# A two-layer trunk in fp32 on one core: every third feed-forward accumulator moved to the small PSUM banks

## The chip, the cores and the metric

The kernel runs on one core of one Trainium2 chip, in one launch. TensorE (PE in the profile, PEld for its weight loads) multiplies into PSUM, eight banks of 512 fp32 columns on each of 128 partitions. VectorE (DVE) and ScalarE (ACT) read the sums from PSUM and write SBUF; GpSimd (POOL) and SyncE (SP) here mostly issue DMAs. The metric is device microseconds of a run; three runs of the kernel before gave a median of 1580.35 us (1576.94 to 1583.97).

## The reference

Two layers work on 640 tokens (512 latent, 128 context) of width 1024. Each layer is an adaLN-modulated RMSNorm, one input projection for three groups of heads (windowed attention, Fourier mixing, latent attention), an output projection with a gated residual, and then the feed-forward, which is what the change touches:

```python
def _conv_ffn(h, w_ug, conv_w, conv_b, w_down):
    u = h @ w_ug                                   # 1024 -> 2 x 2816
    up = jnp.pad(u, ((0, 0), (half, half), (0, 0)))
    uc = sum(up[:, i:i + n] * conv_w[i] for i in range(CONV_W)) + conv_b
    a, g = jnp.split(uc, 2, axis=-1)
    return (jax.nn.silu(g) * a) @ w_down           # 2816 -> 1024
```

The modulation vectors come from `silu(c) @ w_ada + b_ada`, 6144 numbers per layer and condition vector; a part of them is made while the feed-forward runs.

## The kernel before

Activations lie feature-major: a tile is 128 features by 640 tokens. Every fp32 operand is split into a high and a low part (`hh`/`hl`, `th`/`tl`, `wh`/`wl`), and a product is three matmuls (high by high, high by low, low by high), each in two halves of 320 columns, since a bank holds 512. So an accumulator takes two banks, one for each half.

PSUM has two pools. `pmm` holds two tiles "mm" of two banks each; `pss` holds four tiles "s" of one bank each, which serve the attention, the transposes and the row statistics. An `Acc` (line 99) is one "mm" tile, or, with `Acc(False)`, two "s" tiles.

The feed-forward of a layer is the loop at line 338. A step "up" f makes two products, a and g, of feature tile f: eight steps over k, 48 matmuls each. `conv` (line 1278) takes each from PSUM: VectorE multiplies it by the row statistic `r` into `u` (line 1282), ScalarE copies two edge columns (line 1284), which is the last read of the bank, and then come the bias `bb`, the middle tap `y` on ScalarE and the two outer taps on VectorE (line 1292). After g, ScalarE makes the SiLU, VectorE the product `z`, and both split it into `th` and `tl`. A step "down" comes after one more "up" and multiplies a group of six feature tiles (the last group: four) into eight output tiles, 36 matmuls each; `resid` (line 533) adds each to `x` on VectorE in three instructions, the first and only reads of the bank. In the text an accumulator is called a0, g0, a1, g1, ... for the up products and d0 to d7 for the eight output tiles of a down group.

Weights come by DMA in units of up to 128 x 1024 (`wr`, two buffers), and ScalarE and VectorE split each into `wh` and `wl` (lines 186 and 188, four buffers each). VectorE has one more duty in the feed-forward: `ada_dve` (line 350) makes 48 rows of modulations in layer 0 and 8 in layer 1, two reductions over 1024 elements per row ("junk", line 364). The tuple `CFG[l]["ada"]` says how many are asked for after each up step; in layer 0 also each output tile of a down step asks for one, in layer 1 all eight are done by then.

The order on each engine is set by the framework's scheduler, which walks the program by priority with a cost table of its own and gives out the pools' buffers as they come free in its own time. Each engine then runs its list strictly in order and waits by semaphores. At the end of a layer the last down group runs by halves of tokens (`tail`, line 604): in between, `Norm.sums` (line 433) adds the squares by three small matmuls, ScalarE and VectorE make the inverse root (`rc`, line 376), VectorE puts it on a diagonal (`diag`, line 382), and `Norm.spread` (line 442) broadcasts it by three more matmuls. The next layer's first product needs that.

Of the kernel before, what the change touches and what calls it, by code (L numbers as in the profile page):

```python
# [21 lines left out]
HF = 320  # L22
# [56 lines left out]
def hybrid_step(ctx: ExitStack, tc: tile.TileContext, I, O):  # L79
    nc = tc.nc  # L80
# [12 lines left out]
    def MM():  # L93
        return pmm.tile([128, 2, 512], F32, tag="mm", name="mm")

    def PS():
        return pss.tile([128, 512], F32, tag="s", name="s")

    class Acc:


        def __init__(s, wide=True, hfs=(0, 1)):
            s.wide = wide
            if wide:
                s.t = MM()
                s.h = [s.t[:, hf, :] for hf in range(2)]
            else:
                s.h = [PS()[:, :HF] if hf in hfs else None for hf in range(2)]

        def pieces(s):  # L110
            if s.wide:
                return [(s.t[:, :, :HF], halves)]
            return [(s.h[hf], lambda ap, hf=hf: ap[:, hf * HF:(hf + 1) * HF]) for hf in range(2)]

    def SM(name, w=4, bufs=4):
        return sm.tile([128, w], F32, tag=name, name=name, bufs=bufs)
# [1 line left out]
    def halves(ap):  # L118
        return ap.rearrange("p (a b) -> p a b", a=2)
# [4 lines left out]
    def acopy(out, in_):  # L124
        return nc.scalar.activation(out, in_, AF.Copy)  # L125
# [133 lines left out]
    def P(l, n):  # L259
        return pk[l][:, PK[n][0]:PK[n][1]]  # L260
# [972 lines left out]
    if True:  # L1233
# [18 lines left out]
        nrm = Norm(x, 0, 0)  # L1252
# [3 lines left out]
        for l in range(L):  # L1256
            u = U[l]

            def begun():
                x.clear()  # L1260
                i = nc.vector.tensor_scalar_mul(nsink[:, l], P(l, "sink"), -1.0)
                if l:
                    tc.keep_in_program_order(i)

            xn, nrm = mixer(l, nrm, begun, I["xT"] if l == 0 else xd)


            hs = nrm.hs()
            cv = P(l, "conv").rearrange("p (t q) -> p t q", q=4)
            T = {}  # L1270
            bg = ada_dve(0, [(0, n) for n in range(40, 48)] + [(1, n) for n in range(40)]) if l == 0 else ada_dve(48, [(1, n) for n in range(40, 48)])
            made = 0

            nws = SM("nws", 2 * NFT, 1)
            nc.vector.reduce_sum(out=nws, in_=cv[:, :, 0:3], axis=AX.X)
            nc.vector.tensor_scalar_mul(nws, nws, -1.0)

            def conv(ps, t):
                uu = S("u", w=UW)
                for c0, c1, o, p in ((0, NL, 0, 1), (CX, NT, 256, 515)):  # L1280
                    n = c1 - c0
                    nc.vector.tensor_mul(halves(uu[:, p:p + n]), ps.t[:, :, o:o + n // 2], halves(nrm.r[:, c0:c1]))  # L1282
                for v, o in enumerate((uu[:, 0:514:513], uu[:, 514:644:129])):
                    acopy(o, ps.t[:, 1, HF + v:HF + v + 1].to_broadcast([128, 2]))
                bb = SM("bb", 2)
                nc.vector.scalar_tensor_tensor(out=bb, in0=uu[:, 513:515], scalar=nws[:, t:t + 1], in1=cv[:, t, 3:4].to_broadcast([128, 2]), op0=ALU.mult, op1=ALU.add)  # L1286
                y = S("y", w=UW)
                for v, (c0, c1) in enumerate(((0, 513), (513, TW))):
                    nc.scalar.activation(y[:, c0:c1], uu[:, c0 + 1:c1 + 1], AF.Identity, bias=bb[:, v:v + 1], scale=cv[:, t, 1:2])  # L1289
                yy = y[:, :TW]  # L1290
                for q in (0, 2):
                    nc.vector.scalar_tensor_tensor(out=yy, in0=uu[:, q:q + TW], scalar=cv[:, t, q:q + 1], in1=yy, op0=ALU.mult, op1=ALU.add)  # L1292
                return yy

            ya = {}

            def cb_a(f):
                def go(ps):
                    ya[f] = conv(ps, 2 * f)
                return go  # L1300

            def cb_g(f):
                def go(ps):
                    y = conv(ps, 2 * f + 1)
                    a = ya.pop(f)
                    nc.scalar.activation(y, y, AF.Silu)  # L1306
                    if f == NFT - 1:
                        nc.scalar.activation(SM("root", 1, 1), y[:, 1:2], AF.Sqrt, bias=eps[:, 0:1], scale=0.0)
                    z = S("z")
                    for c0, c1, o in ((0, NL, 0), (CX, NT, 2)):  # L1310
                        nc.vector.tensor_mul(z[:, c0:c1], a[:, c0 + o:c1 + o], y[:, c0 + o:c1 + o])
                    T[f] = tuple(S(n, F32R) for n in ("th", "tl"))
                    hilo(T[f][0], T[f][1], z)
                return go

            fin = l == L - 1
            nxt = Norm(xn, None if fin else l + 1, 0)
            if fin:
                yout = {}

                def hfin(hf, c):
                    if c not in yout:
                        yout[c] = S("yo")
                    sl = slice(hf * HF, (hf + 1) * HF)
                    nc.vector.scalar_tensor_tensor(out=yout[c][:, sl], in0=xn[c][:, sl], scalar=P(0, "gfin")[:, c:c + 1], in1=nxt.r[hf][:, :HF], op0=ALU.mult, op1=ALU.mult)  # L1325
                    nc.sync.dma_start(out=O["y"][c, :, sl], in_=yout[c][:, sl])

            def upd_d(last):
                def go(c, ps, hfs):
                    resid(xn[c], ps, l, 5, c, hfs)  # L1330
                    if last:
                        for hf in hfs:
                            nxt.sq(c, hf)
                        if not fin and 1 in hfs:
                            nc.gpsimd.dma_start(out=xd[c], in_=xn[c])
                return go

            for kind, a in u["plan"]:
                if kind == "up":
                    for q, cb in (("a", cb_a(a)), ("g", cb_g(a))):  # L1340
                        ps = Acc()
                        drain(dense(W.get(u[q, a]), hs, range(8), ps, True, True, n=UW))
                        cb(ps)
                    for _ in range(CFG[l]["ada"][a] if a < len(CFG[l]["ada"]) else 0):
                        made += next(bg, 0)
                    continue
                while made < 8:
                    made += next(bg)
                f0, f1 = GROUPS[a]
                nk = f1 - f0  # L1350
                ts = tuple({k: T[f0 + k][q] for k in range(nk)} for q in range(2))
                last = a == len(GROUPS) - 1
                up = upd_d(last)
                if not last:
                    for c in range(8):
                        ps = Acc()
                        drain(dense(W.get(u["d", a, c]), ts, range(nk), ps, True, True))
                        up(c, ps, (0, 1))
                        next(bg, None)
                else:  # L1360
                    drain(bg)
                    accs = [Acc(), Acc(), Acc(False)]
                    for ks in (range(nk - 1), range(nk - 1, nk)):
                        for c in range(3):
                            drain(dense(W.get(u["dl", c // 2]), ts, ks, accs[c], ks[0] == 0, ks[0] != 0, off=(c % 2) * nk))
                            if ks[0]:
                                up(c, accs[c], (0, 1))
                    ps = Acc()
                    drain(dense(W.get(u["dl", 1]), ts, range(nk), ps, True, True, off=nk))
                    up(3, ps, (0, 1))  # L1370
                    items = [(c, W.get(u["dl", c // 2], 3 - c // 4), range(nk), (c % 2) * nk) for c in range(4, 8)]
                    done = 0
                    for i in tail(nxt, items, ts, up):
                        upto = CFG[l]["next"][i]
                        for c in range(done, upto):
                            if fin:
                                hfin(0, c)
                            else:
                                nxt.h(0, c)
                        done = upto  # L1380
                    if fin:
                        nxt.stats(1)
                        for c in range(done, 8):
                            hfin(0, c)
                        for c in range(8):
                            hfin(1, c)
                for f in range(f0, f1):
                    T.pop(f)
            nrm = nxt
# [123 lines left out]
```

## Time and profile before

| | us |
|---|---|
| median of three runs | 1580.35 |
| the profiled execution | 1582.09 |
| its span, first to last instruction | 1580.3 |
| TensorE matmul busy | 1525.2 (97%) |
| VectorE busy | 1116.7 (71%) |
| ScalarE busy | 712.3 (45%) |
| mean granted TensorE clock | 0.984 |

The span goes, in order, through the mixer of layer 0 (to about 340 us), its feed-forward (to about 788), the last down group and the change of layers (to about 820), the mixer of layer 1 (to about 1090), its feed-forward (to about 1545) and the end. TensorE's busy share is near the whole span, and a matmul's row overlaps the next one's, so the rows to look for are those where TensorE was idle before an instruction, and who released it. The clock column is the share of full speed that was granted.

### The profile page before, as it was taken

What the parts mean: (1) busy time and instruction counts of PE and PEld (TensorE: products, weight loads), DVE (VectorE), ACT (ScalarE), POOL (GpSimd) and SP (SyncE); (2) the same over time, 40 slices, a digit from 0 to 9 for tenths busy, and PEclk for the clock granted to TensorE, in tenths of its full rate; (3) what the DMA queues carried; (4) which work ended last, traced back from release to release, by engine and by line L of the source; (5) the groups of instructions that cost most, each with busy time, mean ns of one, the idle gap of its engine ahead of it and who ended that gap; (6) DMA issues with size and microseconds to landing.
All of it is one profiled execution on the core that took longest, in us unless ns stands there. A gap on an engine that the chain in (4) does not pass through costs nothing. (4 is left out here: it accounts for less than half of the span.)

```text
span 1580.3 us, 25827 instructions
## 1 busy us (share of the span) xinstructions
PE 1525.2 (97%) x10082; PEld 1426.3 (90%) x10082; DVE 1116.7 (71%) x2257; ACT 712.3 (45%) x1403; POOL 103.7 (7%) x225
## 2 busy tenths in 40 slices
PE   9999989899999999999999999989999999999997
PEld 7977775599999999999999887869999999999997
DVE  5765674477897888889778777867885466466366
ACT  4555664564432432441445666646433243244142
POOL 1200111100000000001011000120000000000000
PEclk9999999899999999999999999999999999999998
DMA  9542239113334335235244202331332222221211
GB/s 363 166 145 74 73 98 312 56 54 120 116 124 169 120 104 196 104 104 193 81 142 133 72 25 86 114 142 54 120 99 75 81 74 61 94 77 52 100 54 67
DMA packets 61800, 177.59 MB, mean 112 GB/s; under 512 B 7360, under 2 KB 9856, under 8 KB 61680
## 3 DMA queue, kind: packets, MB, share of 16 engines
q1 hardware_dynamic: 44112, 116.41, 22.1%
q0 software_dynamic: 17568, 59.55, 11.2%
q8 instruction: 79, 1.29, 0.3%
q14 instruction: 41, 0.34, 0.1%
HBM read 165.02 MB, written 10.91 MB: 111 GB/s over the span
## 5 line engine op out<-in xcount | busy, mean ns | idle before, releaser
L278 PE MATMUL mm<-hh,wh 128*128 128x320 f32 x1632 | 377.5, 312 | 12.3 <-ACT u L125 9.1
L278 PE MATMUL mm<-hl,wh 128*128 128x320 f32 x1632 | 377.2, 310 | 0.7 <-DVE hl L486 0.4
L278 PE MATMUL mm<-hh,wl 128*128 128x320 f32 x1632 | 376.9, 310 | 0.0
L125 ACT ACTIVATE wh<-wr 128x1024 fp32r<-128x1024 f32 (+2 forms) x189 | 185.9, 984 | 343.1 <-PE mm L278 263.9
L278 PEld LDWEIGHTS mm<-hh,wh 128*128 128x128 f32 x1632 | 273.8, 188 | 20.6 <-ACT u L125 11.0
L278 PEld LDWEIGHTS mm<-hl,wh 128*128 128x128 f32 x1632 | 275.6, 188 | 4.0 <-issue 2.1
L278 PEld LDWEIGHTS mm<-hh,wl 128*128 128x128 f32 x1632 | 274.5, 188 | 3.3 <-issue 3.3
L188 DVE TENSOR_TENSOR wl<-wr,wh 128x1024 fp32r<-128x1024 f32 (+2 forms) x187 | 210.9, 1128 | 48.2 <-ACT wh L125 47.3
L1292 DVE SCALAR_TENSOR_TENSOR y<-u,pk,y 128x642 f32<-128x642 f32 x176 | 156.2, 887 | 67.9 <-ACT y L1289 64.2
L278 PE MATMUL mm<-th,wh 128*128 128x320 f32 x656 | 152.4, 310 | 0.0
L278 PE MATMUL mm<-th,wl 128*128 128x320 f32 x656 | 152.2, 309 | 0.0
L278 PE MATMUL mm<-tl,wh 128*128 128x320 f32 x656 | 152.0, 309 | 0.0
L537 DVE SCALAR_TENSOR_TENSOR x<-mm,mod,x 128x192 f32<-128x192 f32 (+2 forms) x222 | 84.9, 435 | 70.6 <-PE mm L278 70.6
L364 DVE CUSTOM_DVE_ANT_0 junk<-wa,sbc 128x1024 bf16<-128x1024 f32 x112 | 132.1, 1223 | 1.8 <-DMA wa<-in_wat 1.8
L1289 ACT ACTIVATE y<-u,bb,pk 128x513 f32<-128x513 f32 (+1 forms) x176 | 105.9, 650 | 60.8 <-DVE bb L1286 60.8
L278 PEld LDWEIGHTS mm<-th,wh 128*128 128x128 f32 x656 | 110.3, 188 | 0.7 <-ACT th L125 0.4
L278 PEld LDWEIGHTS mm<-th,wl 128*128 128x128 f32 x656 | 110.4, 188 | 0.0
L278 PEld LDWEIGHTS mm<-tl,wh 128*128 128x128 f32 x656 | 110.4, 188 | 0.0
L1282 DVE TENSOR_TENSOR u<-mm,r 128x512 f32<-128x512 f32 (+1 forms) x176 | 79.6, 486 | 42.2 <-PE mm L278 40.1
L125 ACT ACTIVATE u<-mm 128x2 f32<-128x2 f32 x176 | 20.8, 170 | 112.5 <-DVE u L1282 107.5
L1306 ACT ACTIVATE y<-y 128x642 f32<-128x642 f32 x44 | 32.6, 741 | 73.7 <-DVE y L1292 73.7
L361 POOL DMA_DIRECT2D wa<-in_wat x56 | 29.5, 528 | 524.2 <-DVE mod L364 517.8
(311 smaller groups left out, 2195.6 us busy)
## 6 DMA issues: line engine op xcount, KB each, us to landing
wr<-in_wug SPq DMA_DIRECT2D x88, 512.0 KB, 3.5
wa<-in_wat POOLq DMA_DIRECT2D x56, 512.0 KB, 3.8
wa<-in_wa SPq DMA_DIRECT2D x80, 256.0 KB, 5.7
wr<-in_wdn SPq DMA_DIRECT2D x48, 384.0 KB, 3.1
wr<-in_wi SPq DMA_DIRECT2D x16, 512.0 KB, 3.7
wr<-in_wo SPq DMA_DIRECT2D x14, 512.0 KB, 3.7
xpart<-xp POOLq DMA_DIRECT2D x16, 320.0 KB, 3.7
x<-xpart POOLq DMA_DIRECT2D x16, 320.0 KB, 6.1
```

The lines of the kernel that those rows point to most:

```text
L125: return nc.scalar.activation(out, in_, AF.Copy)
L188: pin(self.eng.tensor_sub(lo, r, f32(hi)), fix)
L278: pin(nc.tensor.matmul(ps.h[hf][:, :c1 - c0], lhsT=w[wi][:, off[k] if isinstance(off, dict) else k + off, :], rhs=hs[hi][k][:, c0:c1], sta ...
L361: nc.gpsimd.dma_start(out=t, in_=I["wat"][i0 + i])
L364: nc.vector.tensor_tensor_reduce(out=junk, in0=t, in1=sb[v], scale=1.0, scalar=0.0, op0=ALU.mult, op1=ALU.add, accum_out=mod[l][:, n, v:v ...
L537: nc.vector.scalar_tensor_tensor(out=xc[:, c0:c1], in0=ps.h[hf][:, o:o + c1 - c0], scalar=mod[l][:, gidx * 8 + c, v:v + 1], in1=xc[:, c0:c ...
L1282: nc.vector.tensor_mul(halves(uu[:, p:p + n]), ps.t[:, :, o:o + n // 2], halves(nrm.r[:, c0:c1]))
L1289: nc.scalar.activation(y[:, c0:c1], uu[:, c0 + 1:c1 + 1], AF.Identity, bias=bb[:, v:v + 1], scale=cv[:, t, 1:2])
L1292: nc.vector.scalar_tensor_tensor(out=yy, in0=uu[:, q:q + TW], scalar=cv[:, t, q:q + 1], in1=yy, op0=ALU.mult, op1=ALU.add)
L1306: nc.scalar.activation(y, y, AF.Silu)
```

## The change

In the feed-forward, the accumulators of the up steps and of the first three down groups now come from a counter `FA`: two of three are an "mm" tile as before, every third is two "s" tiles. That is 68 accumulators per layer, of which 22 are of the new kind (14 of up steps, 8 of down steps). For these `conv` reads two tiles, so its two multiplications (512 and 128 columns, both halves in one access pattern) become four (two of 256, two of 64). The last down group keeps its own `Acc` calls. `Acc` now keeps whole "s" tiles, because the edge columns lie behind column 320.

```diff
             else:
-                s.h = [PS()[:, :HF] if hf in hfs else None for hf in range(2)]
+                s.h = [PS() if hf in hfs else None for hf in range(2)]
...
-            return [(s.h[hf], lambda ap, hf=hf: ap[:, hf * HF:(hf + 1) * HF]) for hf in range(2)]
+            return [(s.h[hf][:, :HF], lambda ap, hf=hf: ap[:, hf * HF:(hf + 1) * HF]) for hf in range(2)]
...
                     n = c1 - c0
-                    nc.vector.tensor_mul(halves(uu[:, p:p + n]), ps.t[:, :, o:o + n // 2], halves(nrm.r[:, c0:c1]))
+                    if ps.wide:
+                        nc.vector.tensor_mul(halves(uu[:, p:p + n]), ps.t[:, :, o:o + n // 2], halves(nrm.r[:, c0:c1]))
+                    else:
+                        for hf in range(2):
+                            d = hf * n // 2
+                            nc.vector.tensor_mul(uu[:, p + d:p + d + n // 2], ps.h[hf][:, o:o + n // 2], nrm.r[:, c0 + d:c0 + d + n // 2])
                 for v, o in enumerate((uu[:, 0:514:513], uu[:, 514:644:129])):
-                    acopy(o, ps.t[:, 1, HF + v:HF + v + 1].to_broadcast([128, 2]))
+                    acopy(o, ps.h[1][:, HF + v:HF + v + 1].to_broadcast([128, 2]))
...
+            bank = [0]
+
+            def FA():
+
+                bank[0] += 1
+                return Acc(bank[0] % 3 != 0)
...
                     for q, cb in (("a", cb_a(a)), ("g", cb_g(a))):
-                        ps = Acc()
+                        ps = FA()
...
                     for c in range(8):
-                        ps = Acc()
+                        ps = FA()
```

The scheduler's lists move too, though the program text around the change does not. Three places follow; line numbers of the changed kernel are a few higher (1282 there is 1283 and 1287).

VectorE in the first down group of layer 0, the stretch that ends with the split of the weights of d5. Before, it comes after the residual of d1 (`x` is the residual, "ISA junk" a reduction, `wl` the split):

```order
L144 TENSOR_TENSOR tl<-z,th 128x640
L364 ISA junk,mod_87<-wa,sbc 128x1024
L364 ISA mod_87 128x1
L364 ISA junk,mod_87<-wa,sbc 128x1024
L364 ISA mod_87 128x1
L364 ISA junk,mod_87<-wa,sbc 128x1024
L364 ISA mod_87 128x1
L364 ISA junk,mod_87<-wa,sbc 128x1024
L364 ISA mod_87 128x1
L537 SCALAR_TENSOR_TENSOR x<-mm,mod_86,x 128x320
L537 SCALAR_TENSOR_TENSOR x<-mm,mod_86,x 128x192
L537 SCALAR_TENSOR_TENSOR x<-mm,mod_86,x 128x128
```

The next row there is the `wl` of d5. In the change the same four reductions and the residual of d1 come first, and the list goes on like this, with the residuals of d2 ("mm") and d3 ("s"):

```order
L537 SCALAR_TENSOR_TENSOR x<-mm,mod_86,x 128x192
L537 SCALAR_TENSOR_TENSOR x<-mm,mod_86,x 128x128
L364 ISA junk,mod_87<-wa,sbc 128x1024
L364 ISA mod_87 128x1
L364 ISA junk,mod_87<-wa,sbc 128x1024
L364 ISA mod_87 128x1
L537 SCALAR_TENSOR_TENSOR x<-s,mod_86,x 128x320
L537 SCALAR_TENSOR_TENSOR x<-s,mod_86,x 128x192
L537 SCALAR_TENSOR_TENSOR x<-s,mod_86,x 128x128
L364 ISA junk,mod_87<-wa,sbc 128x1024
L364 ISA mod_87 128x1
L364 ISA junk,mod_87<-wa,sbc 128x1024
```

The `wl` of d5 stands right behind this last reduction: it has moved back by two residuals and six reductions. The second and third down group of layer 0 show nearly the same list.

TensorE at the change of layers, from the sums of squares on; before:

```order
L436 MATMUL s<-ones,acc 128x2 x3
L278 MATMUL mm<-th,wl 128x320
L278 MATMUL mm<-th,wh 128x320
L278 MATMUL mm<-tl,wh 128x320
L278 MATMUL mm<-th,wl 128x320
L383 MATMUL s<-diag,ones 128x128
```

Now:

```order
L278 MATMUL mm<-th,wl 128x320
L278 MATMUL mm<-th,wh 128x320
L278 MATMUL mm<-tl,wh 128x320
L278 MATMUL mm<-th,wl 128x320
L436 MATMUL s<-ones,acc 128x2 x3
L383 MATMUL s<-diag,ones 128x128 x2
L383 MATMUL s<-diag,ones 128x64
```

The four matmuls that stood between the sums and the spread have moved ahead of the sums, and the eight that stood between the spread's first and second matmul have moved behind it.

VectorE at the same place; before, the chain from the inverse root (`rc`) to `diag` runs at once:

```order
L537 SCALAR_TENSOR_TENSOR x<-mm,mod_86,x 128x128
L377 RECIPROCAL rc<-rc 128x6
L382 TENSOR_SCALAR diag<-ident,rc 128x128
L429 TENSOR_TENSOR acc<-acc,sq 128x320
L537 SCALAR_TENSOR_TENSOR x<-mm,mod_86,x 128x192
L537 SCALAR_TENSOR_TENSOR x<-mm,mod_86,x 128x128
L382 TENSOR_SCALAR diag<-ident,rc 128x128 x2
L188 TENSOR_TENSOR wl<-wr,wh 128x1024
```

Now:

```order
L537 SCALAR_TENSOR_TENSOR x<-mm,mod_86,x 128x192
L537 SCALAR_TENSOR_TENSOR x<-mm,mod_86,x 128x128
L188 TENSOR_TENSOR wl<-wr,wh 128x1024
L429 TENSOR_TENSOR acc<-acc,sq 128x320
L377 RECIPROCAL rc<-rc 128x6
L429 TENSOR_TENSOR acc<-acc,sq 128x320
L382 TENSOR_SCALAR diag<-ident,rc 128x128 x3
```

The residual, the split of a weight unit and two additions now stand ahead of `diag`.

## Rows read from the trace of the kernel before

**Rows 1.** Page, busy time by engine.
```profile
PE 1525.2 (97%) x10082; PEld 1426.3 (90%) x10082; DVE 1116.7 (71%) x2257; ACT 712.3 (45%) x1403; POOL 103.7 (7%) x225
```

**Rows 2.** Waits, PE and PEld, whole span: total us, times, longest.
```profile
PE mm L278 <- ACT u L125: 9.1, 7, 1.4
...
PEld mm L278 <- ACT u L125: 11.0, 7, 1.7
```

**Rows 3.** Timeline of PE, 371 to 375: start, us, [idle before <-releaser].
```profile
371.68 0.46 PE L278 MATMUL mm<-hl,wh 128*128 128x320 f32 x2
371.97 0.45 PE L278 MATMUL mm<-hh,wl 128*128 128x320 f32 x2
373.86 0.57 PE L278 MATMUL mm<-hh,wh 128*128 128x320 f32 x2 [1.44 <-ACT u L125]
374.26 0.46 PE L278 MATMUL mm<-hl,wh 128*128 128x320 f32 x2
```

**Rows 4.** Timeline of DVE and ACT in the same stretch.
```profile
368.07 1.22 DVE L364 CUSTOM_DVE_ANT_0 junk<-wa,sbc 128x1024 bf16<-128x1024 f32 x1
...
372.65 0.89 DVE L1282 TENSOR_TENSOR u<-mm,r 128x512 f32<-128x512 f32 x2
...
372.17 1.06 ACT L125 ACTIVATE wh<-wr 128x1024 fp32r<-128x1024 f32 x1 [5.38 <-PE mm L278]
```

**Rows 5.** Windows, both feed-forwards: us; PE, PEld, DVE, ACT, POOL busy; PEclk; DMA.
```profile
340.00:785.00 445.00, 439.73 (x2990) 438.69 (x2990) 365.07 (x636) 165.21 (x295) 24.27 (x46) 1.00 0.38 128
1092.00:1540.00 448.00, 444.13 (x3013) 443.29 (x3012) 278.90 (x470) 167.24 (x297) 3.17 (x6) 1.00 0.24 81
```

**Rows 6.** Lines by form, VectorE, line 1282: busy us, mean ns.
```profile
L1282 DVE TENSOR_TENSOR u<-mm,r 128x512 f32<-128x512 f32 x88 | 60.7, 689 | 42.2 <-PE mm L278 40.1 <-ACT r L125 2.0
...
L1282 DVE TENSOR_TENSOR u<-mm,r 128x128 f32<-128x128 f32 x88 | 24.9, 283 | 0.0
```

**Rows 7.** Timeline of DVE, first down group of layer 0.
```profile
446.05 0.69 DVE L1282 TENSOR_TENSOR u<-mm,r 128x512 f32<-128x512 f32 x1 [1.02 <-PE mm L278]
...
449.94 1.81 DVE L1292 SCALAR_TENSOR_TENSOR y<-u,pk,y 128x642 f32<-128x642 f32 x2 [0.40 <-ACT y L1289]
...
455.29 1.22 DVE L364 CUSTOM_DVE_ANT_0 junk<-wa,sbc 128x1024 bf16<-128x1024 f32 x1
...
459.87 1.14 DVE L537 SCALAR_TENSOR_TENSOR x<-mm,mod,x 128x320 f32<-128x320 f32 x3
460.91 0.96 DVE L188 TENSOR_TENSOR wl<-wr,wh 128x768 fp32r<-128x768 f32 x1
...
475.47 1.23 DVE L364 CUSTOM_DVE_ANT_0 junk<-wa,sbc 128x1024 bf16<-128x1024 f32 x1 [0.44 <-DMA wa<-in_wat]
```

**Rows 8.** Timeline of PE, then DVE, at the change of layers.
```profile
812.31 0.73 PE L436 MATMUL s<-ones,acc 128*128 128x2 f32 x6
...
813.94 0.49 PE L383 MATMUL s<-diag,ones 128*128 128x128 f32 x2 [0.21 <-DVE diag L382]
...
819.64 0.56 PE L278 MATMUL mm<-hh,wh 128*128 128x320 f32 x2 [1.24 <-ACT hh L468]
...
813.37 0.19 DVE L377 RECIPROCAL rc<-rc 128x6 f32<-128x6 f32 x1 [0.96 <-ACT rc L376]
...
813.80 0.49 DVE L429 TENSOR_TENSOR acc<-acc,sq 128x320 f32<-128x320 f32 x1
814.20 0.67 DVE L537 SCALAR_TENSOR_TENSOR x<-mm,mod,x 128x192 f32<-128x192 f32 x2
...
815.17 1.22 DVE L188 TENSOR_TENSOR wl<-wr,wh 128x1024 fp32r<-128x1024 f32 x1
```

**Rows 9.** PE idle in the mixer of layer 0, and windows there: PE busy, PEclk.
```profile
282.69 1.48 PE L286 MATMUL mm<-CKb,CQ 96*128 96x320 f32 x5 [2.04 <-ACT P L1105]
...
282.00:288.00 6.00, 5.31 (x27) 0.72 0.00 0
302.00:312.00 10.00, 7.95 (x38) 0.66 0.46 176
```

## The prediction, on record before the changed kernel ran

> **What bounds the kernel now.** The page comes first: TensorE is busy for 1525.2 of 1580.3 us [rows 1], so the change can give back only what TensorE loses by waiting, and the matmuls themselves are as many as before. The view of waits says where that is. In the feed-forwards there is one kind of any size: the first matmul of an accumulator waits for ScalarE's edge copy `u`, the last read of the bank that it wants. That happens 7 times, 9.1 us of idle matmul queue, or 11.0 us seen from the weight loads [rows 2].
>
> The timeline shows what such a wait costs. Pairs of matmuls start every 0.29 us (371.68, 371.97); the next starts at 373.86, which is 1.89 later, and the one after it needs 0.40 instead of 0.29 [rows 3]. So 1.60 + 0.11 = 1.7 us are lost where the row says 1.44, and that is why the weight loads' 11.0 us are the better sum for all seven.
>
> Next, why the bank was late. The accumulator a1 was complete when g1 began, about 365.2 (g1 ends at 372.27, less 24 pairs of 0.295, 7.07 us). But VectorE was in four reductions from 368.07 to 372.65, and only then took a1 out of its bank [rows 4]. With two accumulators, a2 wants a1's bank just when g1 is done: TensorE has 7.07 us of patience, and VectorE came after 7.45. The places fit the program: the tuple asks for two rows of reductions at once after up steps 0, 4, 9 and 15 of layer 0 and 0, 2 and 4 of layer 1, seven in all. Elsewhere TensorE does not wait, and VectorE is busy for 365 of 445 us in layer 0 and 279 of 448 in layer 1 [rows 5]: late at places, not too slow.
>
> **The change part by part.** *A third accumulator.* With two of three on "mm", an "mm" tile is wanted again by the third accumulator after it, so its readers have two whole products, 14.1 us, instead of 7.07; an "s" pair is wanted six later. The longest that a reader took, about 8.6 us (365.2 to the restart at 373.86), fits with 5 us to spare. All seven waits go: -11.0 us. What could be late next is the weights, and in the up steps they are not: ScalarE's split waits for TensorE to free one of the four buffers [rows 4], so weights are as far ahead as the buffers allow.
>
> *Four multiplications for two.* 512 columns take 689 ns and 128 take 283 [rows 6], so a column costs (689 - 283) / 384 = 1.06 ns and an instruction 148 ns before its first column. 28 up accumulators (14 a layer) with two more instructions each are 8.3 us of VectorE, spread over 893 us in which it has 249 us free. On the path: 0, covered by the 14.1 us. If a place had no cover it would cost 0.3 us there.
>
> *The down groups of layer 0.* Here the moved list matters. The weights of d5 are now split behind the residuals of d2 and d3 and six more reductions. I count from the end E of g6 on TensorE (before: 446.0, [rows 7]). TensorE begins d5 after five outputs of 18 pairs, E + 26.5. Before, the split was done at 460.91 + 0.96 = E + 15.9, over 10 us early. Now VectorE can begin with the residual of d0 at E + 5.35. The nine instructions from there to `tl` are the same as those from 449.94 to 455.29, 5.35 us; as the split no longer stands between `z` and `tl`, `tl` waits for ScalarE's `th`, an estimate of 0.8 (ScalarE's split of 1024 columns takes 1.06 [rows 4], this one has 640): E + 11.5. Four reductions, 4.58 (455.29 to 459.87): 16.1. The residual of d1, 1.04: 17.1. Then d2 with two reductions, 1.04 + 2.29, two more, 2.29, d3, 1.04, two more, 2.29: E + 25.8 to 26.1. The split itself, 0.96: E + 26.9. TensorE is 0.4 us late, and with a restart like that of rows 3 it loses 0.7. The other two groups have nearly the same list: 3 x 0.7 = +2.1 us. It is a small difference of two large sums: at best nothing is late (0), and with a reduction that waits for its DMA (0.44 in [rows 7]) and as much error again in the sum, 2 us each (6.0). I take 2.1, the sum itself. In layer 1 the reductions are over by then: 0.
>
> *The change of layers.* Before, TensorE did four matmuls between the sums and the spread and idled 0.21 us; the sums began at 812.31, the reciprocal at 813.37, the spread at 813.94 [rows 8]. Now the spread follows the sums at once, and VectorE has more ahead of it. From the start S of the sums: the residual of the product just ended, from 0.2, takes 0.6 (814.20 to 814.79 or so); the split 1.14; an addition 0.4 (813.80 to 814.20); the reciprocal 0.23; an addition 0.4; the diagonal 0.25: S + 3.2. The sums are done at S + 0.6, so TensorE idles 2.6 us. Part of that is not lost, because before it idled 1.24 us at 819.64 for `hh` [rows 8]. S is now 0.6 later (four matmuls moved ahead), 812.9; spread at 816.1, done at 816.7; twelve matmuls to 818.5; the residual, `ht` and `hh` behind them, 0.6 + 0.5 + 0.6 us: the next layer begins at about 820.3, 0.65 late, and with the weight split that now stands between two of its first steps 0.9. That is the price by the chain alone.
>
> An idle of this length also touches the clock. After the 2.04 us of idle before 282.69 the granted clock was at its lower level for a while, a mean of 0.72 over 6 us, 1.7 us of lost work; around another such idle it was 0.66 over 10 us, 3.4 us [rows 9]. The feed-forward windows with the waits of up to 1.44 us stand at 1.00 [rows 5]. So I add 1.7: 0.9 + 1.7 = +2.6. The bounds are 0.6 (no fall, the split hidden) and 0.9 + 3.4 = 4.3.
>
> [...]
>
> Sum: -11.0 + 2.1 + 2.6 = -6.3 us. Against the profiled execution's 1582.09 us (span 1580.3 and 1.8 around it) that is 1575.8. The profiled run lies 1.7 above the median of the three runs, so as a median I expect 1580.35 - 6.3 = 1574.0 us.
>
> **The rivals.** *Both prices stay hidden.* The first split is late by only 0.4 us of 26.9, and the idle at the layers' change could end up in the 1.24 that was there. Then the seven waits are the whole story: 1580.35 - 11.0 = 1569.4, or 1570 with the chain's 0.6. For it: the sums for the prices are as small as their errors. Against: the moved lists are there, and every idle over 2 us that I looked at was followed by the lower clock.
>
> *The waits only change their name.* If VectorE's reductions delayed the next weights or `tl` as much as the bank, TensorE would stop at the same seven places, and the time would stay at 1580. For it: the split of a unit stands right behind the late `u`. Against: ScalarE's wait for a free weight buffer [rows 4], three units of lead.
>
> *Slower: the clock falls in the down groups.* VectorE gets to the split of d5 at E + 28.3 instead of 26.9, for instance by one more DMA wait and one more late residual. TensorE then idles about 2 us, which is where the rows show the clock fall, in each of three groups: 3 x (2.1 + 3.4) = 16.5, and the change of layers costs its upper bound, 4.3: 1580.35 - 11.0 + 16.5 + 4.3 = 1590. It decides from an idle of 2 us on, that is from 1.4 us more delay than I count. Against: each output adds only 1.04 + 2.29 + 0.87 = 4.2 us to VectorE in TensorE's 5.3, so a delay shrinks again and does not build up.
>
> **How the numbers follow.** About 0.5%, 7.9 us, is what a measurement of this kernel can tell from no change. The forecast, 1574.0, gets 0.50, with a range of its own of 1571 to 1578; hidden prices, 1569.4, 0.25; waits that change their name, 1580, 0.18; slower, 1590, 0.07. Faster by more than 0.5% means below 1572.4: all of the second case and a fifth of the first, 0.35. Slower means above 1588.3: most of the last, 0.05. The rest, 0.60, is within. The range runs from 1567 (hidden prices and 2 us of scatter between runs) to 1582 (the same waits under another name); it leaves out the slow case and the tails.
>
> **What would show it.** Right: no row of PE in the feed-forwards that waits for ScalarE's `u`; in layer 0 three short waits of PE for `wl`, 0.3 to 1 us, at the fifth or sixth output of each of the first three down groups, none in layer 1; a wait of 2 to 3 us for `diag` at the change of layers with the clock below 1.00 behind it. Wrong: `u` still in the waits, waits for `wl` in the up steps, or idles of 2 us in the down groups.

## The result, and the profile after

The changed kernel took 1572.9 us, the median of seven runs (1569.57 to 1573.79), beside 1580.41 of the kernel before on the same chip: a ratio of 0.9947, with a 95% interval of 0.9933 to 0.9961. That is -8.4 us (-10.6 to -6.2). The forecast was 1574.0, -6.3. Measured once more in the last experiment, the change came to 0.9957 (0.9939 to 0.9976), -6.8 us.

TensorE's idle time in the profile fell from 55.1 to 48.4 us (span less busy time); the rest of the difference is busy time. It was longer at the lower granted clock: the second profile of the changed kernel has the same idle time within 1 us (49.2) at a mean granted clock of 0.982 instead of 0.988, and 1524.4 us busy instead of 1519.4. The page's row of busy time, and the windows of the two feed-forwards (us; PE, PEld, DVE, ACT, POOL busy; granted clock; DMA), which answer to [rows 1] and [rows 5]:

```profile
PE 1519.4 (97%) x10082; PEld 1422.0 (91%) x10082; DVE 1118.0 (71%) x2313; ACT 709.8 (45%) x1403; POOL 103.4 (7%) x225
...
340.00:785.00 445.00, 444.39 (x3022) 443.33 (x3021) 368.69 (x667) 164.29 (x298) 24.27 (x46) 1.00 0.38 128
1085.00:1540.00 455.00, 455.00 (x3097) 454.67 (x3096) 287.82 (x515) 173.41 (x309) 3.17 (x6) 1.00 0.24 79
```

In the feed-forwards TensorE is now busy for 444.4 of 445 us and 455 of 455. The seven waits for `u` [rows 2] are gone from PE's waits. The same view for PEld (total us, times, longest), first the whole span and then the feed-forward of layer 0, shows what stands in their place. The one wait for `u` that is left there, 0.3 us, comes at 784.04, behind the up steps; PE's own row shows no idle for it.

```profile
PEld s L383 <- DVE diag L382: 3.8, 2, 2.9
...
PEld mm L278 <- DVE wl L188: 1.4, 3, 0.8
...
PEld mm L278 <- ACT u L125: 0.3, 1, 0.3
```

The three waits for `wl` are one in each of the first three down groups, as the weight loads' timeline (start, us, what waited) shows:

```profile
468.53 0.30 PEld L278 LDWEIGHTS mm<-th,wl 128*128 128x128 f32 x2 [0.27 <-DVE wl L188]
...
596.46 0.30 PEld L278 LDWEIGHTS mm<-th,wl 128*128 128x128 f32 x2 [0.78 <-DVE wl L188]
...
728.76 0.30 PEld L278 LDWEIGHTS mm<-th,wl 128*128 128x128 f32 x2 [0.34 <-DVE wl L188]
```

The change of layers, PE first and then DVE, answers to [rows 8]:

```profile
806.44 0.81 PE L436 MATMUL s<-ones,acc 128*128 128x2 f32 x6
810.06 0.88 PE L383 MATMUL s<-diag,ones 128*128 128x128 f32 x6 [2.81 <-DVE diag L382]
810.75 0.39 PE L278 MATMUL s<-th,wh 128*128 128x320 f32 x1
...
814.21 0.30 PE L278 MATMUL s<-th,wl 128*128 128x320 f32 x1
814.58 0.56 PE L278 MATMUL mm<-hh,wh 128*128 128x320 f32 x2
...
806.64 0.68 DVE L537 SCALAR_TENSOR_TENSOR x<-mm,mod,x 128x192 f32<-128x192 f32 x2 [0.28 <-PE mm L278]
807.58 1.22 DVE L188 TENSOR_TENSOR wl<-wr,wh 128x1024 fp32r<-128x1024 f32 x1 [0.27 <-ACT wh L125]
808.73 0.48 DVE L429 TENSOR_TENSOR acc<-acc,sq 128x320 f32<-128x320 f32 x1
809.13 0.18 DVE L377 RECIPROCAL rc<-rc 128x6 f32<-128x6 f32 x1
809.31 0.49 DVE L429 TENSOR_TENSOR acc<-acc,sq 128x320 f32<-128x320 f32 x1
809.72 0.67 DVE L382 TENSOR_SCALAR diag<-ident,rc 128x128 f32<-128x128 f32 x3
```

TensorE idles 2.81 us for `diag`, behind the residual, the split and the two additions on VectorE. After the spread all 24 last matmuls follow without a pause, and the wait for `hh` (1.24 before) is gone.

Where the time went, by five points of TensorE's timeline: the first matmul of each feed-forward, the sums of squares at the end of each layer, and layer 1's first matmul. The sums stand 0.59 us (four matmuls) later in the changed list; the table takes that off the feed-forward and puts it to the change of layers. The last column is the second profile of the changed kernel.

| stretch, us | before | after | difference | after, again |
|---|---|---|---|---|
| mixer of layer 0 | 341.74 | 339.70 | -2.04 | 341.18 |
| feed-forward of layer 0 | 470.57 | 466.15 | -4.42 | 465.78 |
| change of layers | 7.33 | 8.73 | +1.40 | 11.10 |
| mixer of layer 1 | 271.48 | 269.77 | -1.71 | 272.12 |
| feed-forward of layer 1 | 469.16 | 463.72 | -5.44 | 463.73 |
| end | 20.02 | 19.73 | -0.29 | 19.69 |
| span | 1580.3 | 1567.8 | -12.5 | 1573.6 |

The two profiles alone would say -12.5, 4 us more than the runs. The mixers make up 3.75 of that, where nothing was changed: the granted clock fell in them in both profiles, to a mean of 0.96 over the mixer of layer 0 in each, and of 0.97 before and 0.99 after over that of layer 1. In the windows before and after round the same place of layer 1's mixer it is 0.90 and 0.95 (us; PE busy, granted clock, DMA):

```profile
940.00:975.00 35.00, 33.64 (x196) 0.90 0.23 75
```

```profile
934.00:969.00 35.00, 33.31 (x201) 0.95 0.23 74
```

The second profile of the changed kernel has a longer mixer in layer 1 than before has. What belongs to the change is -4.42 + 1.40 - 5.44 = -8.5 us in the first profile and -4.79 + 3.77 - 5.43 = -6.5 in the second, beside -8.4 and -6.8 of the runs. Each is one execution against the one profile of before, so the agreement is no closer than the clock's price at the change of layers allows (below).

### The profile page after: what moved, and what is told of

It is laid out like the page before. It is cut to its first block, busy times and chain, and to the rows that moved or that the text cites. A ratio compares the mean times of both kernels' runs of the same rounds, so it can differ in the third digit from the quotient of the medians.

```text
span 1567.8 us, 25828 instructions
## 1 busy us (share of the span) xinstructions
PE 1519.4 (97%) x10082; PEld 1422.0 (91%) x10082; DVE 1118.0 (71%) x2313; ACT 709.8 (45%) x1403; POOL 103.4 (7%) x225
## 5 line engine op out<-in xcount | busy, mean ns | idle before, releaser
L278 PE MATMUL mm<-hl,wh 128*128 128x320 f32 (+1 forms) x1184 | 275.0, 310 | 0.9 <-DVE hl L469 0.5
L278 PE MATMUL mm<-hh,wh 128*128 128x320 f32 (+1 forms) x1184 | 273.7, 311 | 1.8 <-ACT wh L125 0.9
L278 PE MATMUL mm<-hh,wl 128*128 128x320 f32 (+1 forms) x1184 | 274.3, 310 | 0.0
L278 PEld LDWEIGHTS mm<-hl,wh 128*128 128x128 f32 x1184 | 199.9, 188 | 4.2 <-issue 2.1
L278 PE MATMUL s<-hh,wh 128*128 128x320 f32 x480 | 111.1, 310 | 0.0
L278 PE MATMUL s<-hh,wl 128*128 128x320 f32 x480 | 111.0, 309 | 0.0
L278 PE MATMUL s<-hl,wh 128*128 128x320 f32 x480 | 110.8, 309 | 0.0
L537 DVE SCALAR_TENSOR_TENSOR x<-mm,mod,x 128x320 f32<-128x320 f32 (+1 forms) x174 | 66.5, 432 | 48.6 <-PE mm L278 48.4
L278 PEld LDWEIGHTS s<-hl,wh 128*128 128x128 f32 x480 | 81.0, 188 | 0.0
L278 PEld LDWEIGHTS s<-hh,wh 128*128 128x128 f32 x480 | 80.9, 188 | 0.0
L278 PEld LDWEIGHTS s<-hh,wl 128*128 128x128 f32 x480 | 80.7, 188 | 0.0
```

The costliest lines, as they stand in the source:

```text
L278: pin(nc.tensor.matmul(ps.h[hf][:, :c1 - c0], lhsT=w[wi][:, off[k] if isinstance(off, dict) else k + off, :], rhs=hs[hi][k][:, c0:c1], sta ...
L537: nc.vector.scalar_tensor_tensor(out=xc[:, c0:c1], in0=ps.h[hf][:, o:o + c1 - c0], scalar=mod[l][:, gidx * 8 + c, v:v + 1], in1=xc[:, c0:c ...
```

## The experiments

| run | what it is | ratio to before, 95% interval |
|---|---|---|
| e1 | third accumulator in layer 1 alone | 0.9990 (0.9975 to 1.0004) |
| e2 | in layer 0 alone | 0.9988 (0.9972 to 1.0004) |
| e3 | before, reductions replaced by a copy | 0.9970 (0.9953 to 0.9986) |
| e4 | changed kernel, the same | 0.9938 (0.9916 to 0.9960) |
| e9 | before, reductions replaced by a memset | 0.9935 (0.9914 to 0.9955) |
| e5 | before, reductions handed out singly | 0.9952 (0.9934 to 0.9969) |
| e6 | changed kernel, all 88 products split | 0.9958 (0.9944 to 0.9972) |
| e7 | changed kernel, longer idle | 1571.87 us, one run |
| e8 | e5 with the sums asked for earlier | 0.9949 (0.9931 to 0.9967) |
| e10 | singly, and earlier; two accumulators | 0.9932 (0.9912 to 0.9953) |
| e11 | the same with the third accumulator | 0.9932 (0.9910 to 0.9953) |
| e12 | the changed kernel again | 0.9957 (0.9939 to 0.9976) |

### One layer at a time (e1, e2)

```diff
-                return Acc(bank[0] % 3 != 0)
+                return Acc(l != 1 or bank[0] % 3 != 0)
```

(e2: `l != 0`.)

> The third accumulator in the feed-forward of layer 1 alone; layer 0 and the change of layers keep the order of before. Theory A (the gain is the waits for a late bank and nothing else, the extra multiplications are covered): the three waits for u at the start of layer 1's feed-forward go, the four of layer 0 stay, no wait for wl is added; -5.4 us, 0.9966 of before. Rival B (the gain comes from the new order as a whole or from the clock): the time does not follow the waits; anything from 1.000 to 0.995.

> The third accumulator in the feed-forward of layer 0 alone, with the new order at the change of layers. Theory A: the four waits for u of layer 0 go, three waits of weight loads for wl (1.4 us in all) and the wait of 2.8 us for diag stand as in the changed kernel; layer 0's feed-forward is 6.5 us shorter, the change of layers 1.4 longer, so -5.1 us, 0.9968 of before, and the three waits of layer 1 stay. Rival B: the sum of this and the run on layer 1 alone differs from the change's 8.4 us by more than 3 us.

The waits came as theory A had them. PE's waits in the two feed-forwards and the change of layers between them, e1 and then e2:

```profile
PE mm L278 <- ACT u L125: 5.3, 4, 1.4
```

```profile
PE mm L278 <- ACT u L125: 3.9, 3, 1.4
PE s L383 <- DVE diag L382: 2.8, 1, 2.8
...
PE mm L278 <- DVE wl L188: 0.4, 1, 0.4
```

In e1 the four waits of layer 0 stay and layer 1's feed-forward takes 464.52 us (469.16 before, -4.6; -5.4 was expected). In e2 the three of layer 1 stay, and layer 0's feed-forward is 4.6 shorter (466.60 less 0.59, against 470.57; 6.5 was expected). The run times did not follow as well. In e2's profile the clock fell after the idle for `diag` (a window of 0.86, below), the change of layers took 9.70 + 0.59 = 10.29 us, 3.0 more than before, and -4.6 + 3.0 = -1.6 lies beside the measured -1.9 (-4.4 to +0.6). That is consistent, but does not show why the median came out there: the profiled execution (1572.48 us) was the fastest of the twelve, its mixer of layer 0 5 us shorter than before's, and without the fall -4.6 + 1.4 = -3.2 would lie in the interval as well. For e1 -4.6 was to be had, and -1.6 (-3.9 to +0.6) was measured. Its profile shows no new wait that would take the 3 us; the mixer of layer 0 was 1.8 longer in it, and at the change of layers its clock fell (0.89 in the window from 814 to 826). By the letter of rival B (the two runs add up to more than 3 us less than the change) B stands; by the rows, and by e5, e9 and e10 below, A does. What slowed e1's runs, and with it this part of B, stays open.

### Without the reductions (e3, e4, e9)

```diff
-            for v in range(2):
-                junk = sp.tile([128, 1024], BF16, tag="S", name="junk")
-                nc.vector.tensor_tensor_reduce(...)
+            nc.vector.tensor_copy(mod[l][:, n, :], t[:, 0:2])   # e3, e4
+            nc.vector.memset(mod[l][:, n, :], 0.0)              # e9
```

> The kernel before with the two reductions of every modulation row in the feed-forwards left out (a copy of two numbers stands for them, so those modulations are not computed; their DMAs stay). Theory A (two accumulators are enough wherever VectorE has no block of four reductions): no wait for u is left, no wait for wl, the change of layers as before: -11.0 us, 0.993. Rival C (u is late by VectorE's whole load, the blocks only make it show): some of the seven waits stay at less than 1.7 us each, 0.995 to 0.999.

> The changed kernel with the same reductions left out. Theory A: the third accumulator has nothing left to give, so the same as the kernel before without reductions within 0.1% (0.993 of before), with no wait for u or wl in either feed-forward; the four multiplications for two cost nothing. Rival D (an accumulator in two small banks costs something of its own, in restarts or in multiplications): 0.5 us or more in each feed-forward, 0.994 or above, against the kernel before without reductions.

> The kernel before with the reductions left out and a memset in their place that reads no row (so those modulations are zero), in place of the copy that waited for the row's DMA in the earlier run without reductions. Theory A (two accumulators are enough when VectorE is not held up): no wait for u in either feed-forward, the change of layers as before, so layer 0's feed-forward about 464.8 us to the sums (before 470.6), layer 1's 463.9 (before 469.2): -11 us, 0.993 of before. Rival C (VectorE's load as a whole): waits for u remain.

e3 missed its forecast for a reason of its own, and a useful one. Two waits for `u` stayed in its layer 0. DVE's timeline shows that the copies, with no reductions to take up the time, stood waiting for their rows' DMA, and held up all behind them; the two PE rows are what came of it, and the clock fell around the longer one (window from 398 to 412: 0.76):

```profile
383.62 0.17 DVE L362 COPY mod<-wa 128x2 f32<-128x2 f32 x1 [2.18 <-DMA wa<-in_wat]
...
400.67 0.17 DVE L362 COPY mod<-wa 128x2 f32<-128x2 f32 x1 [2.78 <-DMA wa<-in_wat]
...
386.87 0.56 PE L278 MATMUL mm<-hh,wh 128*128 128x320 f32 x2 [1.34 <-ACT u L125]
403.93 0.91 PE L278 MATMUL mm<-hh,wh 128*128 128x320 f32 x2 [2.64 <-ACT u L125]
```

e4 had the same copies and the same stalls, one of them longer, and TensorE did not wait in that place:

```profile
398.18 0.17 DVE L362 COPY mod<-wa 128x2 f32<-128x2 f32 x1 [3.67 <-DMA wa<-in_wat]
```

So the third accumulator covered a VectorE that was late by a DMA as well as one that was late by reductions. It was not complete: against the expectation one wait for `u` of 0.2 us stayed in e4's feed-forward of layer 0. In e9, where nothing reads the row, two accumulators have no wait in either feed-forward (464.35 and 463.88 us), and 0.9935 is the expected 0.993. e4's 0.9938 is the same within the noise (its feed-forwards take 464.99 and 463.91), so with the reductions gone the third accumulator gives nothing, and rival D's price in each feed-forward is not there. It is the reductions that make the bank late. Whether their blocks do it or the load that they add (rival C) e9 cannot tell, since it takes away both; e5 and e10 can.

### Reductions one at a time, two accumulators (e5, e8, e10), and with the third (e11)

```diff
-CFG[0]["ada"] = (3, 1, 1, 1, 2, 1, 1, 1, 1, 2, 1, 1, 1, 1, 1, 2, 1, 1, 1, 1)
+CFG[0]["ada"] = (4, 3, 3, 3, 2, 2, 2, 2, 2, 2, 2, 2, 2, 2, 2, 2, 2, 2, 2, 2, 2, 2)   # e5, e8
+CFG[0]["ada"] = (4, 3, 3, 3, 3, 3, 3, 3, 3, 3, 3, 3, 2, 2, 2, 2, 2, 2, 0, 0, 0, 0)   # e10, e11
-CFG[1]["ada"] = (3, 1, 2, 1, 2)
+CFG[1]["ada"] = (4, 3, 3, 3, 2, 2)
-CFG[0]["tail"] = (1, 2)
+CFG[0]["tail"] = (0, 1)   # e8 alone
...
             for v in range(2):
+                if v:
+                    yield 0.5
...
-            yield 1
+            yield 0.5
...
-                    for _ in range(CFG[l]["ada"][a] if a < len(CFG[l]["ada"]) else 0):
-                        made += next(bg, 0)
+                        w = CFG[l]["ada"][a] if a < len(CFG[l]["ada"]) else 0
+                        for _ in range(w // 2 if q == "a" else w - w // 2):
+                            made += next(bg, 0)
...
                         next(bg, None)
+                        next(bg, None)
```

> The kernel before, all accumulators as there, but the reductions handed out one at a time: after each a and each g product, mostly one, never more than two together, and the first eight rows done by up step 5. Theory A: with no block of four VectorE is never later than the 7.07 us of patience, so all seven waits go without another bank: -11.0 us in the feed-forwards; the order at the change of layers comes out like that of the changed kernel, +1.4: 0.994 of before, as the change itself. No waits for wl in the down groups, so up to 2 us better than the change. Rival C (VectorE's load as a whole): waits for u remain, some in new places, 0.997 or above.

> The spread reductions on two banks as before (one at a time), and the sums and the spread of the last down group asked for one item earlier (tail 0, 1 instead of 1, 2), which puts the reciprocal ahead of one addition and the three diagonals ahead of another on VectorE. Theory A: the wait for diag falls from 2.8 to about 2.0 us; the way from the sums to layer 1's first matmul is 0.8 us shorter than in the run without this, the rest the same: 0.9935 of before. Rival: what diag gains hh loses, no difference within 0.1%.

> The kernel before, two accumulators, with the reductions handed out one at a time as in the earlier run, but more of them in the early up steps and none in the last four, which leaves the order at the change of layers as it was before (four matmuls between the sums and the spread, the diagonal ahead of the weight split). Theory A: no wait for u, none for wl, diag 0.2 us and hh 1.24 us as before, clock 1.00 there: -11 us, 0.993 of before, 2.5 us better than the changed kernel. Rival: a wait in a new place in the down groups, where the first rows are wanted, or the price at the change of layers is not the clock's and the time stays at the change's 0.995.

> The same hand-out of reductions, with the third accumulator of the change on top. Theory A: nothing is left for it to give, the same time as two accumulators with this hand-out within 0.1%. Rival G (the third accumulator also covers what the replay of one profile does not show, a late DMA or a slow VectorE place): 1 us or more better than two accumulators.

e5 has no wait of PE for `u` or `wl` with before's banks and all of before's reductions, so rival C falls: the block is what counts. The feed-forwards take 465.11 (465.70 less 0.59) and 463.88 us. It pays at the change of layers, where its list is that of the changed kernel, and comes out where the change does; the 2 us that it might have been better are not there. e8 moved the reciprocal ahead there: the idle is 1.95 us instead of 2.46, and the way from the sums to layer 1's first matmul 8.61 instead of 9.27, 0.66 of the expected 0.8. That is too little for the runs to tell, which gave 0.9949 where 0.9935 was expected. e10 kept before's order there. PE's rows at the change of layers, with the pause for `diag` back at 0.21:

```profile
804.73 0.74 PE L438 MATMUL s<-ones,acc 128*128 128x2 f32 x6
806.37 0.49 PE L385 MATMUL s<-diag,ones 128*128 128x128 f32 x2 [0.21 <-DVE diag L384]
...
812.05 0.56 PE L278 MATMUL mm<-hh,wh 128*128 128x320 f32 x2 [1.24 <-ACT hh L470]
```

7.32 us, as before (7.33), and 0.9932: the expected 0.993, -11 us. e11, the third accumulator on top, has the same ratio. With no block left it gave nothing that shows (it has one wait for `wl` of 0.47 us in layer 0), and nothing speaks for rival G, though a gain of 1 us is too small for six runs to exclude. e10 and e11 have the best ratios of all that compute the whole. That they beat before is measured. Against the change itself, in the same comparison, the medians are 1569.6 and 1569.72 against 1573.07; the intervals of the ratios (0.9957 for the change) overlap, so that they beat the change is likely, not settled.

### All 88 products with split multiplications (e6)

```diff
-                    if ps.wide:
+                    if False:
                         nc.vector.tensor_mul(halves(uu[:, p:p + n]), ps.t[:, :, o:o + n // 2], halves(nrm.r[:, c0:c1]))
```

> The changed kernel with the four multiplications for two in all 88 up products instead of 28: 120 more instructions, 120 x 148 ns = 17.8 us more of VectorE, twice what the change added. Theory A (they lie in the 14.1 us that a reader has): no wait for u, the time of the change within 0.2%, at most some tenths more at the three waits for wl. Rival D (each has a price on the path): 0.15 to 0.3 us for each of 60 products, 9 to 18 us slower than the change, 1.000 to 1.006 of before.

0.9958 lies within 0.2% of the change, with no wait for `u` (and none for `wl`, where the change had three): the instructions are off the path, and rival D falls. Their size is as worked out; lines by form of the changed kernel (busy us, mean ns):

```profile
L1283 DVE TENSOR_TENSOR u<-mm,r 128x512 f32<-128x512 f32 x60 | 41.2, 687 | 22.8 <-PE mm L278 20.8 <-ACT r L125 2.0
L1287 DVE TENSOR_TENSOR u<-s,r 128x256 f32<-128x256 f32 x56 | 21.0, 418 | 8.6 <-PE s L278 8.5
L1283 DVE TENSOR_TENSOR u<-mm,r 128x128 f32<-128x128 f32 x60 | 16.8, 280 | 0.0
L1287 DVE TENSOR_TENSOR u<-s,r 128x64 f32<-128x64 f32 x56 | 9.7, 213 | 0.0
```

2 x 418 - 687 = 149 ns and 2 x 213 - 280 = 146 ns more for each split (148 was the estimate).

### The clock at the change of layers (e7, e12)

```diff
             rstd(self.rc[hf], ps[:, 0:6], 1024)
+            if hf == 0 and self.l == 1:
+                for _ in range(12):
+                    nc.vector.tensor_scalar_mul(self.rc[hf], self.rc[hf], 1.0)
```

> The changed kernel with twelve more small VectorE instructions (a multiplication of rc by one) in the chain to diag at the change of layers, about 2.3 us, so that TensorE idles about 5.1 us there instead of 2.8. Theory E (the granted clock falls at this place as in the mixers, only a longer idle is needed after matmuls without a pause): a granted clock below 1.00 behind the idle and 2.3 + 1.7 us or more on the way from the sums to layer 1's first matmul, 12.7 us or more instead of 8.7. Rival F (a single idle in a stretch of dense matmuls does not lower it, at this length either): clock 1.00, 11.0 us.

> The changed kernel once more, beside the three others on one chip. Theory A: 0.9947 of before as first measured; its profile shows after the wait of 2.8 us for diag either a granted clock of 1.00, as the first profile did, or 0.50 for a while, as the run on layer 0 alone did, and the way from the sums to layer 1's first matmul is 8.1 us in the first case and 9.7 or 10.6 in the second.

The windows round this place (us; PE busy, granted clock, DMA): the change's first profile, e2, e12 and e6, all four with the same order and an idle of 2.8 us, then e7 with 5.28:

```profile
806.00:818.00 12.00, 8.64 (x56) 1.00 0.36 130
```

```profile
803.00:815.00 12.00, 8.92 (x49) 0.86 0.31 115
```

```profile
807.00:819.00 12.00, 8.85 (x44) 0.72 0.31 115
```

```profile
805.00:817.00 12.00, 9.19 (x46) 0.72 0.30 109
```

```profile
804.00:818.00 14.00, 8.47 (x46) 0.76 0.25 92
```

The same idle was followed by a window at 1.00 once and by windows at 0.86, 0.72 and 0.72, where the clock was down once for a shorter and twice for a longer while. The way from the sums to layer 1's first matmul followed: 8.14, 9.70, 10.51 and 10.60 us. In e7 it was 12.29, or 12.88 with the four matmuls, as theory E had it, at 0.76; F falls. Its idle is 2.5 us longer than e12's, and its way 1.8. That a longer idle is needed, as E says, is not so: the clock fell after 2.8 us as well, and after 1.95 us in e8 (0.86; the last section).

## Why the prediction was right, point by point

*The waits.* All seven went, and nothing took their place in the up steps. Layer 1 alone gave 5.44 and 5.43 us in the two profiles, where 4.7 of the weight loads' 11.0 us [rows 2] had stood. Layer 0 gave 4.42 and 4.79, net of the waits for `wl`. The sum of both layers, -9.9 and -10.2, was forecast as -11.0 + 2.1 = -8.9. Layer 1's 5.44 is more than its waits: e1, with the same accumulators there, gave 4.64, and kernels without a wait differ by as much as the rest (the last section), so that part was not forecast and has no cause on record. That a bank made late by a block of four reductions is the cause, and not VectorE's load, is shown by e5 and e10, which do all the reductions and have no wait for `u` with two accumulators; e9 shows that without reductions there is none.

*The multiplications.* 0 on the path, shown by e6 with 88 products split instead of 28.

*The down groups.* Three waits, one in each of the first three groups, none in layer 1, 0.27, 0.78 and 0.34 us: the place was right, and the sum is 1.4 us by the weight loads instead of 2.1 (PE's own rows show the middle one alone, 0.51). At 468.53 TensorE waits for the split of VectorE that stands behind the residual of d3 and two reductions (DVE, then PE, first down group):

```profile
463.84 1.13 DVE L537 SCALAR_TENSOR_TENSOR x<-s,mod,x 128x320 f32<-128x320 f32 x3
465.23 1.23 DVE L364 CUSTOM_DVE_ANT_0 junk<-wa,sbc 128x1024 bf16<-128x1024 f32 x1 [0.26 <-DMA wa<-in_wat]
...
467.53 0.95 DVE L188 TENSOR_TENSOR wl<-wr,wh 128x768 fp32r<-128x768 f32 x1
...
467.34 0.46 PE L278 MATMUL mm<-th,wh 128*128 128x320 f32 x2
467.63 0.46 PE L278 MATMUL mm<-tl,wh 128*128 128x320 f32 x2
467.93 0.46 PE L278 MATMUL s<-th,wh 128*128 128x320 f32 x2
...
468.54 0.56 PE L278 MATMUL mm<-th,wl 128*128 128x320 f32 x2
```

That the size came out is in part luck, for two errors nearly cancel here. The split was done at 468.48, 27.4 us after g6's end (441.06), not 26.9: two of the reductions ahead of it waited for their DMA, 0.49 us together. And TensorE does not need `wl` when d5 begins: d5 began at 467.34, 26.3 after g6's end (forecast 26.5), but its first two pairs read `wh`, two of d6 follow, and the first that reads `wl` comes 1.2 us later. Set against d5's beginning, as in the prediction, the split would have been 1.1 us late, not 0.4.

*The change of layers.* The chain up to `diag` was right: VectorE began the diagonals 3.28 us after the sums (806.44 to 809.72), 0.27 of it a wait for `wh`; the forecast had the first one finished at 3.2. The idle is 2.81, forecast 2.6. What follows was miscounted. "Twelve matmuls to 818.5" were 24: the eight that had stood between the spread's parts, and the sixteen that had followed it. That takes the wait for `hh` away in full and still costs +1.40 instead of 0.9, at full clock. The clock's 1.7 us was right as a size between cases: 0 in the first profile, 9.70 - 8.14 = 1.6 in e2, 10.51 - 8.14 = 2.4 in e12, 2.5 in e6. The whole place costs 1.4 to 3.9, forecast 2.6 within 0.6 to 4.3. The reason given, that every idle over 2 us had been followed by the lower clock, is not a rule: the first profile's 2.81 us was not, and in three of six profiles with before's order the clock fell (0.86 to 0.89), in e1 and e9 with no idle over 1.24 us. So the order before had a price too, at which the prediction put nothing, and that the term came out near the mean of the four is in part luck.

*The sum.* -6.3 was forecast, -8.4 and -6.8 measured, so the median fell into the forecast's own range of 1571 to 1578. The feed-forwards gave 1.0 and 1.3 us more than forecast, 0.7 of it in the down groups; the change of layers came out 1.2 cheaper in one profile and 1.2 dearer in the other. "Hidden prices" is out, since the waits for `wl` and the longer change of layers stand in the trace (the clock's part of it in three of four profiles); "the waits only change their name" is out, since no wait of that size is in the up steps; "slower" is out, since the down groups' idles stay under 1 us at clock 1.00. That the price which this rival put on a longer idle is real shows in e3, where the clock stood at 0.76 in the window around an idle of 2.64 us in a feed-forward. The ratio, 0.5% faster, lies on the border between two of the three chances, and its repeat, 0.4%, on the other side of it.

*Three accumulators in turn.* They stood at clock 1.00 in the windows of both feed-forwards. They left hardly a pause there (0.6 us idle in 445), so this trace shows the going round itself at full clock, and nothing of what longer pauses would have done.

## What to carry to other kernels

A wait for a buffer can be taken away at either end: by another buffer, which here covered a reader late by a DMA too (e4), or by breaking up the block of work that makes the reader late (e10), after which the buffer gave nothing more (e11). Where a scheduler makes the order, look at every place where the lists differ, also away from the edit: a seventh to over a third of what the feed-forwards gave back was lost at the change of layers, where nothing had been edited. And compare stretch by stretch: two profiles differed by 4 us in mixers that were the same in both kernels.

## What the runs showed of the hardware

In these profiles the length of TensorE's idle did not settle alone whether the granted clock fell. Thirteen of them, by the order at the change of layers; the number is the mean clock of a window of 12 us there (e7: 14):

| idles there | granted clock 1.00 | fell: 0.86 to 0.89 | fell: 0.72 to 0.76 |
|---|---|---|---|
| 2.8 us for `diag` | the change, first profile | e2 0.86 | e6 0.72, e12 0.72 |
| 2.46 (e5), 1.95 (e8), 5.28 (e7) for `diag` | | e5 0.86, e8 0.86 | e7 0.76 |
| 0.21 for `diag`, 1.24 for `hh` | before, e10, e11 | e1 0.89, e4 0.86, e9 0.87 | |

(e11 stands there by its rows: 3.62 us from layer 1's first matmul to the next sums, where before and e10 took 3.63 and e9 4.85. e4 stands there by its window, with 1.76 us of idle in all as in e9's.)

After the same 2.8 us it stood at 1.00 once and fell three times. With before's order it stood at 1.00 three times and fell three times; in e9 it stood at 0.71 from 812.5 to 818, about layer 1's first matmul (813.56). In e4 (window from 806 to 818):

```profile
806.00:818.00 12.00, 10.24 (x58) 0.86 0.61 195
```

That is 0.14 of 12 us, 1.7 us of lost work, which the stretches above count in the mixer of layer 1. What else decides is not shown.

Nor did the kernels without a wait take the same time to the tenth: layer 1's feed-forward, with no wait of TensorE after its first matmul, took 463.72 us in the change, 463.88 in e9 and 465.42 in e10, up to 0.4% apart. Here this went with the kernel and not with the execution: the change's second profile took 463.73. In e10 pairs of matmuls start 0.2949 us after one another in the mean, against 0.2938 in the change, and they do so in nine of ten equal parts of the stretch; no row shows a cause.
